# One burst of TensorE work per mLSTM chunk and per attention row block in a hybrid decoder layer on one Trainium2 core

## The chip, the cores and the metric

The kernel runs on one core of a Trainium2 chip. The core's engines work side by side, each through its own queue of instructions in order: TensorE (PE, matmuls and transposes into PSUM; PEld is its loading of weights), VectorE (DVE), ScalarE (ACT), GpSimd (POOL) and SyncE (SP, which issues all the DMAs here). The metric is the device time of one execution in microseconds, the median of the runs; lower is better. In a view, L81 is line 81 of the kernel.

## What is computed

One layer of a decoder over a sequence of 1024 tokens of width 1024, in float32. Two mixers, a differential attention (4 heads, causal, with a distance bias) and an mLSTM (4 heads, in chunks), read one projection of the normalised input; their outputs are gated, merged and projected back. Cut to what matters:

```python
h = _rmsnorm(x, norm_pre[l])
proj = jnp.einsum('bsd,dn->bsn', h, w_in[l])
qa, ka, va, za, qb, kb, vb, ob, zb, igb, fgb, ga, gb = _split(proj, sizes)
...
oa = _diff_attention(qa, ka, va, lam)
oa = _rmsnorm(oa, norm_a[l].reshape(H_A, 2 * HEAD_DIM_A)) * (1.0 - lam_init)
ya = oa.reshape(B, S, W_A) * jax.nn.silu(za)
...
qk = jax.nn.silu(_causal_conv(jnp.concatenate([qb, kb], axis=-1), conv_qk[l]))
hb = _mlstm(qb_c, kb_c, vb, ig, fg)
hb = jax.nn.sigmoid(ob.astype(jnp.float32)).reshape(B, S, H_B, HEAD_DIM_B) * hb
hb = _rmsnorm(hb, norm_b[l].reshape(H_B, HEAD_DIM_B)).astype(x.dtype)
yb = hb.reshape(B, S, W_B) * jax.nn.silu(zb)
merged = (jax.nn.sigmoid(ga) * jnp.einsum('bsw,wd->bsd', ya, w_a[l])
          + jax.nn.sigmoid(gb) * jnp.einsum('bsw,wd->bsd', yb, w_b[l]))
out = jnp.einsum('bsd,de->bse', merged, w_out[l])
x = x + _rmsnorm(out, norm_post[l])
```

Attention: per head two score matrices (queries and keys of 64 each), two softmaxes, `p0 - lam * p1`, then the product with the values. mLSTM: per chunk a decayed score matrix times the values, plus the queries times a running state C, and the update of that state.

## The kernel before, in words

Every float32 operand of the large products is split into a rounded part and a rest (`split`, L114: an ACT cast and a DVE subtraction), and a product takes three matmuls per 128 rows of depth. Small matmuls and all transposes are plain float32.

**Start (L163 to L218, L600 to L622).** WARM = 15 matmuls of ones run while the first loads are under way (L169). `npre` is the pre-norm weight vector on all 128 partitions; one DMA writes it there 128 times over (L172). Eight tiles of 128 tokens are loaded, normalised (`norm_tile`, L203: ACT square sum, DVE, a POOL power, DVE scaling by npre), transposed on PE (`turn_tile`, xT in the views) and split; `tok_pass` multiplies each by a first group of projection columns (`tok`). From tile 4 on, `turn_tile` also forms differences of the blocks, in PSUM's reach on DVE (t1, t2, L259) and, in `rest` (L262), two on POOL (L263, L264), whose splits are ht1 to ht4: the operands of a seven-product scheme of block multiplication.

**Products (L313 to L466).** The other projection columns are done in pairs of column blocks (`Pair`). Each pair needs seven products of 12 matmuls of 512 columns (`product`, L370), written to three PSUM accumulators, with ACT and DVE reading them out (`Banks.after`, L351) and preparing weights two products ahead (`prep`, L412). `run_pairs` (L431) walks over 24 pairs in a list (qkb: mLSTM queries and keys; qka: attention; ob, va: values and gates by token; zb, za, g: gates). In the views the tiles of a pair carry its name and the accumulator X, Y or Z. Behind the products of token-wise pairs, four transposes (tkT) are put off by one product by way of the list `later` (L454, L565). `merge_b` and `merge` (L1063) then multiply the mLSTM's outputs by w_b, 16 runs of 12 matmuls (mrg); the attention's outputs by w_a follow at the end, and then the output projection (out, L1192).

**Weaving (L1027 to L1050).** This product work, called the fill, is a generator: it yields the estimated time of each half product. The dependent chains, gate_chain, conv, mlstm and attn_head, are generators too and yield how much fill is wanted before they go on; `weave` pulls that much. `until(name)` pulls fill until a pair is done. A scheduler below the program may still move instructions a little; the built order is what counts.

**mLSTM (L783 to L887).** 32 chunks of 128 tokens. `lead` does the scores of the next chunk (sT, with kT a transpose of the keys), `follow` the current chunk's numerator and state update (num, upd), each followed by DVE and ACT work. Between lead and follow, and again behind follow, half of MSTEP = 7 us of fill is pulled. The causal convolution of the next head (`conv`, L743: six parts on DVE and ACT) is put behind chunks 2 to 5, one or two parts each.

**Attention (L927 to L1024).** Per head 8 row blocks of 128 queries. `score(i, c)` (two of them: matmuls S, a DVE pass that adds the bias and finds the minimum, L950, an ACT exponential, L957), `combine` (L966 to L971, DVE), `turn` (transposes pT on PE, copied by ACT, L987), `weigh` (pv on PE, read out by ACT, L996). Fill is pulled behind each of score 0, score 1 with combine, turn and weigh, in the parts FW = 1.0, 0.6, 1.3, 1.0 of a row block's share; row block i's turn and weigh come behind the scores of block i + 1. At a head's end POOL scales the rows (`scale_rows`, L719). A pool of five PSUM buffers (`misc`, L92) serves S, pT, pv, sT, kT, num, upd and the transposes.

## Time and profile before

| | us |
|---|---|
| median of 3 runs | 850.76 |
| lowest and highest run | 849.82, 855.57 |
| the profiled execution | 853.26 |
| its span, first to last instruction | 851.5 |
| PE busy in it | 830.5 |
| DVE, ACT, POOL busy in it | 571.5, 399.6, 63.2 |

The profile is of one execution. Busy time of PE counts matmuls whose ends overlap the next one's start, so it is an upper bound of what PE does. A wait is idle time of an engine just before an instruction, put down to what released it. The chain that ended last is followed back from the last instruction; its pieces are cut where the next begins. The granted clock of TensorE is shown as a share of full speed.

### The profile page before, as it was taken

How to read it: one execution, taken by the hardware profiler on the slowest of the kernel's cores; microseconds unless marked ns; L12 is line 12 of the kernel's file. 1: busy time of each engine (PE TensorE's matmuls, PEld its weight loads, DVE VectorE, ACT ScalarE, POOL GpSimd, SP SyncE). 2: the span in 40 equal slices, each digit the busy share in tenths (PEclk: the TensorE clock that was granted, in tenths of full speed). 3: DMA queues.
4: the chain of work that ended last, by engine and by line, in shares of the span. 5: the costliest groups of instructions: out<-in, count | busy, mean ns of one | idle time of the engine just before them, and what ended most of it. 6: DMA issues, size and time to landing. Idle time of an engine off the chain costs nothing.

```text
span 851.5 us, 12166 instructions
## 1 busy us (share of the span) xinstructions
PE 830.5 (98%) x4292; PEld 703.7 (83%) x4292; DVE 571.5 (67%) x1145; ACT 399.6 (47%) x890; POOL 63.2 (7%) x86
## 2 busy tenths in 40 slices
PE   7899999999999999999999999999999999999997
PEld 7898878888888888888888888788877888778885
DVE  6997868868757966666676765777576635782133
ACT  5554544545444544346555555565566422341110
POOL 1330000000000000100001000200200010000011
PEclk9999999999999999999999999999999999999999
DMA  7612433442452556563366416543567577940052
GB/s 267 200 38 76 124 100 105 142 145 76 127 161 75 169 165 188 171 188 123 112 177 198 132 63 205 178 125 99 192 231 255 178 257 258 307 153 1 1 197 99
DMA packets 100621, 128.96 MB, mean 151 GB/s; under 512 B 8680, under 2 KB 60112, under 8 KB 100560
## 3 DMA queue, kind: packets, MB, share of 16 engines
q1 hardware_dynamic: 100560, 128.18, 47.6%
q8 instruction: 34, 0.56, 0.3%
q14 instruction: 27, 0.22, 0.1%
HBM read 88.79 MB, written 39.35 MB: 150 GB/s over the span
## 4 chain that ended last, share of the span: by engine, by line
PE 76%; DVE 10%; DMA 8%; ACT 3%; issue 2%; SPq 1%; POOL 0%; DVEq 0%; POOLq 0%; ACTq 0%
PE out L81 10%; PE mrg L81 6%; PE pv L81 4%; PE S L81 3%; PE pT L84 2%; DMA zs<-z_d 2%; PE num L81 2%; PE tok L81 1%; PE qka1Y L81 1%; PE zb0Y L81 1%; PE g02Y L81 1%; PE za0Y L81 1%; PE g10Y L81 1%; PE qkb1Y L81 1%; PE qkb2Y L81 1%
## 5 line engine op out<-in xcount | busy, mean ns | idle before, releaser
L957 ACT ACTIVATE p<-p,ast 128x128 f32<-128x128 f32 (+7 forms) x64 | 49.7, 776 | 58.7 <-DVE ast L956 35.5
L950 DVE CUSTOM_DVE_ANT_0 p<-S,gm 128x384 f32<-128x384 f32 (+5 forms) x96 | 50.6, 553 | 22.2 <-PE S L81 21.7
L1211 DVE TENSOR_TENSOR o<-out,npost 128x512 f32<-128x512 f32 x16 | 11.1, 691 | 57.0 <-ACT oj L1207 57.0
L81 PE MATMUL mrg<-y,mbw 128*128 128x512 f32 x192 | 47.2, 395 | 0.0
L81 PE MATMUL mrg<-y,maw 128*128 128x512 f32 x192 | 44.0, 390 | 1.9 <-DVE tg L1084 1.9
L81 PEld LDWEIGHTS mrg<-y,maw 128*128 128x128 f32 x192 | 36.0, 188 | 9.7 <-DVE tg L1084 2.3
L1207 ACT ACTIVATE oj<-out 128x512 f32<-128x512 f32 x16 | 9.6, 598 | 69.3 <-PE out L81 69.2
L81 PEld LDWEIGHTS pv<-va,pT 128*128 128x128 f32 x288 | 36.8, 191 | 5.4 <-ACT pT L987 3.1
L81 PEld LDWEIGHTS mrg<-y,mbw 128*128 128x128 f32 x192 | 35.4, 188 | 6.9
L81 PE MATMUL pv<-va,pT 128*128 128x128 f32 x288 | 37.8, 276 | 1.3 <-ACT pT L987 1.2
L81 PE MATMUL S<-kll,qs 128*128 128x384 f32 (+5 forms) x96 | 32.7, 342 | 0.3 <-DMA kll<-qk_d 0.3
L1084 DVE SCALAR_TENSOR_TENSOR tg<-tg,mrg 128x512 f32<-128x512 f32 x32 | 21.9, 683 | 15.8 <-PE mrg L81 15.6
L81 PE MATMUL S<-khh,qs 128*128 128x384 f32 (+5 forms) x96 | 32.4, 340 | 0.0
L750 DVE SCALAR_TENSOR_TENSOR cv<-pad,cols,cv 128x1024 f32<-128x1024 f32 x24 | 30.7, 1280 | 0.1
L971 DVE SCALAR_TENSOR_TENSOR p<-p,ast,p 128x128 f32<-128x128 f32 (+7 forms) x32 | 26.2, 818 | 1.0
L81 PE MATMUL out<-wo,m 128*128 128x512 f32 x96 | 23.1, 389 | 0.0
L851 POOL TENSOR_TENSOR stb<-stb,mhalf 128x4 f32<-128x4 f32 x8 | 10.8, 1351 | 160.8 <-DVE stb L848 160.8
L115 ACT CAST m<-tg 128x512 fp32r<-128x512 f32 x16 | 9.9, 621 | 25.8 <-DVE tg L1155 25.8
L987 ACT COPY pT<-pT 128x512 f32<-128x512 f32 (+3 forms) x48 | 21.0, 472 | 2.0 <-PE pT L84 2.0
L81 PEld LDWEIGHTS S<-kll,qs 128*128 128x128 f32 x96 | 18.0, 188 | 3.8 <-DMA kll<-qk_d 0.5
L81 PEld LDWEIGHTS out<-wo,m 128*128 128x128 f32 x96 | 18.0, 188 | 3.7
L81 PE MATMUL out<-wot2h,m 128*128 128x512 f32 x64 | 21.0, 390 | 0.0
(1237 smaller groups left out, 2499.4 us busy)
## 6 DMA issues: line engine op xcount, KB each, us to landing
raw_g<-in_w_in_dram SPq DMA_DIRECT2D x16, 512.0 KB, 3.9
g_d<-g SPq DMA_DIRECT2D x32, 256.0 KB, 3.5
tg<-g_d SPq DMA_DIRECT2D x32, 256.0 KB, 3.9
raw_qkb<-in_w_in_dram SPq DMA_DIRECT2D x16, 256.0 KB, 3.3
z_d<-zt SPq DMA_DIRECT2D x16, 256.0 KB, 2.6
zs<-z_d SPq DMA_DIRECT2D x16, 256.0 KB, 4.6
raw_qka<-in_w_in_dram SPq DMA_DIRECT2D x16, 256.0 KB, 3.0
qk_d<-qah SPq DMA_DIRECT2D x16, 256.0 KB, 2.1
```

Source lines behind the costliest of these rows:

```text
L81: pin(nc.tensor.matmul(*args, **kw))
L84: pin(nc.tensor.transpose(out=out, in_=in_, identity=ident))
L115: nc.scalar.copy(hi, raw)
L750: nc.vector.scalar_tensor_tensor(out=cv, in0=pad[:, t : t + S], scalar=cols[:, t * 8 + blk : t * 8 + blk + 1], in1=cv, op0=ALU.mult, op1=A ...
L851: nc.gpsimd.tensor_tensor(rr, ss, mhalf[:, 0:4], ALU.pow)
L950: nc.vector.tensor_tensor_reduce(out=pr[:, n0:n1], in0=pss[:, : n1 - n0], in1=gm[:, (7 - i) * P + n0 : (7 - i) * P + n1], scale=-0.125, sc ...
L957: nc.scalar.activation(pr[:, :nk], pr[:, :nk], AF.Exp, bias=nm, scale=-1.0, accum_out=sth[:, c, i : i + 1],)
L971: nc.vector.scalar_tensor_tensor(out=p0[:, :nk], in0=p1[:, :nk], scalar=st[:, 3:4], in1=p0[:, :nk], op0=ALU.mult, op1=ALU.add,)
L987: nc.scalar.copy(pT[:, j0:j1], pt[:, 0 : (j1 - j0) * P].rearrange("p (j t) -> p j t", t=P))
L1084: nc.vector.scalar_tensor_tensor(out=tg, in0=tg, scalar=1.0, in1=ps, op0=ALU.add, op1=ALU.mult)
L1207: nc.scalar.activation(junk, ps, AF.Square, scale=D ** -0.5, accum_out=ssq[:, tt, cc : cc + 1])
L1211: nc.vector.tensor_mul(orr[:, c0 : c0 + 512], ps, npost[:, c0 : c0 + 512])
```

## The change

Six edits. (1) WARM goes from 15 to 8, and the pre-norm weights come as two rows of 512 on one partition, which PE spreads to 128 partitions by a matmul with ones and ACT copies to npre. (2) The two subtractions of `rest` go from POOL to DVE, and so does `scale_rows` of the attention. (3) Transposes put off by `later` wait for four product steps, or two at the next burst, where they join its work. (4) An mLSTM chunk does lead and follow together and then pulls all of its fill; the convolution has one part behind each of chunks 1 to 6. (5) A row block of the attention does weigh of block i - 2, turn of block i - 1 and both scores of block i together, and then pulls all of its fill; a head has ten such steps. (6) `weave` pulls at least 0.6 of what a chain wants, even where `until` has pulled ahead.

```diff
-WARM = 15
+WARM = 8
...
-LAST = 8
-FW = (1.0, 0.6, 1.3, 1.0)
+LAST = 5
...
-    nc.sync.dma_start(npre, norm_pre[0].partition_broadcast(P))
+    for n0 in range(0, D, 512):
+        prow, pn = temp("prow")[0:1, :], misc("npre")
+        nc.sync.dma_start(prow, norm_pre[:, n0 : n0 + 512])
+        nc.tensor.matmul(pn, ones[0:1, :], prow, start=True, stop=True)
+        nc.scalar.copy(npre[:, n0 : n0 + 512], pn)
...
         def rest():
-            nc.gpsimd.tensor_sub(b11, t2, b11)
-            nc.gpsimd.tensor_sub(b21, b21, t2)
+            nc.vector.tensor_sub(b11, t2, b11)
+            nc.vector.tensor_sub(b21, b21, t2)
...
-    later = []
+    fresh, later, tick = [], [], [0]
+
+    def turns(age):
+
+        while later and later[0][0] <= tick[0] - age:
+            later.pop(0)[1]()
...
-            flush, later[:] = later[:], []
             yield from pairs[p].run(i)
-            for f in flush:
-                f()
-            if finished:
-                done.add(finished)
-                finished = None
+            tick[0] = n
+            turns(4)
+            later.extend((n, f) for f in fresh)
+            fresh.clear()
             if i == 6:
-                finished = pairs[p].name
...
+                later.append((n, lambda name=pairs[p].name: done.add(name)))
+        tick[0] += 9
+        turns(0)
...
                 lead(*divmod(n + 1, NT))
-            yield w * 0.5
             follow(h, c)
...
-            if c % 4 == 1 and n > 4:
+            if c % 4 == 2 and n > 4:
...
-                if c == 2:
+                if c == 1:
                     until(f"qkb{h + 1}")
                     conv_next = conv(h + 1)
-                if 2 <= c <= 5:
-                    for _ in range(2 if c in (3, 5) else 1):
-                        next(conv_next, None)
-                if c == 5:
+                if 1 <= c <= 6:
+                    next(conv_next, None)
+                if c == 6:
                     drain(conv_next)
...
-            yield w * 0.5
+            yield w
...
-        unit = supply / FTOTAL
-        for i in range(NT + 1):
-            w = share(i) * unit
+        unit = supply / sum(share(i) for i in range(NT + 2))
+        for i in range(NT + 2):
+            if i > 1:
+                weigh(i - 2)
+            if 0 < i <= NT:
+                turn(i - 1)
             if i < NT:
                 score(i, 0)
-                yield w * FW[0]
                 score(i, 1)
                 combine(i)
-                if i == NT - 1:
-                    after()
-                yield w * FW[1]
-            if i > 0:
-                if i == 1 and before is not None:
-                    flip(*before)
-                turn(i - 1)
-                yield w * FW[2]
-                weigh(i - 1)
-                yield w * FW[3]
+            if i == 1 and before is not None:
+                flip(*before)
+            if i == NT - 1:
+                after()
+            yield share(i) * unit
...
-        scale_rows(raw, rr, nc.gpsimd)
+        scale_rows(raw, rr, nc.vector)
...
         for want in chain:
-            left[0] = pull(left[0] + want)
+            turns(2)
+            due = left[0] + want
+            now = max(due, 0.6 * want)
+            left[0] = pull(now) + due - now
```

How this moves the built order, first on PE in a chunk of the mLSTM's second head, before (kT, num: small work of the chunk; qkb2Y: products of the fill):

```order
L84 MATMUL kT<-ident,cv_1072 128x128
L81 MATMUL qkb2Y<-ht2h,qkb2w_1902 128x512
L81 MATMUL qkb2Y<-ht2l,qkb2w_1902 128x512
L81 MATMUL qkb2Y<-ht2h,qkb2w_1902 128x512 x2
L81 MATMUL qkb2Y<-ht2l,qkb2w_1902 128x512
L81 MATMUL qkb2Y<-ht2h,qkb2w_1902 128x512 x2
L81 MATMUL qkb2Y<-ht2l,qkb2w_1902 128x512
L81 MATMUL qkb2Y<-ht2h,qkb2w_1902 128x512 x2
L81 MATMUL qkb2Y<-ht2l,qkb2w_1902 128x512
L81 MATMUL qkb2Y<-ht2h,qkb2w_1902 128x512
L81 MATMUL num<-vbh,ring 128x129
L81 MATMUL num<-cn,qi 128x129
```

and the same kind of place with the change:

```order
L80 MATMUL qkb2Y<-ht4l,qkb2w_1992 128x512
L80 MATMUL qkb2Y<-ht4h,qkb2w_1992 128x512
L80 MATMUL sT<-cv_1073,cv_1074 128x128
L83 MATMUL kT<-ident,cv_1074 128x128
L80 MATMUL num<-vbh,ring 128x129
L80 MATMUL num<-cn,qi 128x129
L80 MATMUL upd<-vbh,ring 128x129
L80 MATMUL qkb2Y<-ht4h,qkb2w_1992 128x512
L80 MATMUL qkb2Y<-ht4l,qkb2w_1992 128x512
```

The twelve products that stood between kT and num are now on the two sides of one burst of sT, kT, num and upd.

On PE in the last head of the attention, sixth and seventh row block, before (S: scores, pT: transposes, pv: weighing, mrg: the fill):

```order
L81 MATMUL S<-khh_3_5918,qs_3_5916 128x448
L81 MATMUL S<-kll_3_5920,qs_3_5916 128x448
L81 MATMUL S<-khh_3_5918,qs_3_5916 128x448
L81 MATMUL S<-kll_3_5920,qs_3_5916 128x448
L81 MATMUL mrg<-y_6434,mbw_6588 128x512 x3
L81 MATMUL mrg<-y_6439,mbw_6588 128x512 x3
L84 MATMUL pT<-ident,p_6418 128x128 x6
L81 MATMUL mrg<-y_6444,mbw_6588 128x512 x3
L81 MATMUL mrg<-y_6449,mbw_6588 128x512 x3
L81 MATMUL mrg<-y_6434,mbw_6588 128x512 x3
L81 MATMUL mrg<-y_6439,mbw_6588 128x512 x3
L81 MATMUL pv<-va_5921,pT 128x128 x6
```

and with the change, one row block on:

```order
L80 MATMUL mrg<-y_6465,mbw_6562 128x512 x3
L80 MATMUL pv<-va_5909,pT 128x128 x6
L83 MATMUL pT<-ident,p_6512 128x128 x7
L80 MATMUL S<-khh_3_5905,qs_3_5903 128x512
L80 MATMUL S<-kll_3_5907,qs_3_5903 128x512
L80 MATMUL S<-khh_3_5905,qs_3_5903 128x512
L80 MATMUL S<-kll_3_5907,qs_3_5903 128x512
L80 MATMUL S<-khh_3_5906,qs_3_5904 128x512
L80 MATMUL S<-kll_3_5908,qs_3_5904 128x512
L80 MATMUL S<-khh_3_5906,qs_3_5904 128x512
L80 MATMUL S<-kll_3_5908,qs_3_5904 128x512
L80 MATMUL mrg<-y_6470,mbw_6562 128x512 x3
```

Scores, transposes and weighing, which had products between them, stand together, and each reads what the burst before it left.

On DVE at the start, about the third tile of tokens, before (x_171 and x_205: scaling by npre; ht1l: a split; gt, vb: reading out tok; scr: a small reduction):

```order
L260 TENSOR_TENSOR t_0_237<-xT_1_229,t_0_236 128x512
L217 TENSOR_SCALAR xst_208<-xst_208 128x1
L306 COPY vb_0_265<-tok 128x256
L635 ISA scr,lam_s<-scr 128x64
L635 ISA lam_s 128x1
L116 TENSOR_TENSOR ht1l<-t_0_236,ht1h 128x4x128
L220 SCALAR_TENSOR_TENSOR x_171<-x_171,xst_208,npre 128x1024
L217 TENSOR_SCALAR xst_300<-xst_300 128x1
L305 TENSOR_TENSOR gt<-tok,bif 128x8
L306 COPY vb_4_348<-tok 128x256
L220 SCALAR_TENSOR_TENSOR x_205<-x_205,xst_300,npre 128x1024
L116 TENSOR_TENSOR h11l<-xT_0_305,h11h 128x4x128
```

and with the change (x_173 and x_207 are the same tiles, b_0_203 and b_0_204 the subtractions that were POOL's):

```order
L309 COPY vb_0_267<-tok 128x256
L223 SCALAR_TENSOR_TENSOR x_173<-x_173,xst_210,npre 128x1024
L308 TENSOR_TENSOR gt<-tok,bif 128x8
L220 TENSOR_SCALAR xst_302<-xst_302 128x1
L309 COPY vb_4_350<-tok 128x256
L223 SCALAR_TENSOR_TENSOR x_207<-x_207,xst_302,npre 128x1024
L115 TENSOR_TENSOR h11l<-xT_0_307,h11h 128x4x128
L115 TENSOR_TENSOR h21l<-xT_1_314,h21h 128x4x128
L266 TENSOR_TENSOR b_0_203<-t_0_239,b_0_203 128x512
L267 TENSOR_TENSOR b_0_204<-b_0_204,t_0_239 128x512
L115 TENSOR_TENSOR ht2l<-t_0_239,ht2h 128x4x128
L115 TENSOR_TENSOR ht1l<-t_0_238,ht1h 128x4x128
```

The scaling of both next tiles moved ahead of the small reduction and of the split ht1l, and the two subtractions stand behind them.

## Rows read from the trace of the kernel before

**Rows 1.** The page, first part: busy us, share, instructions by engine.

```profile
PE 830.5 (98%) x4292; PEld 703.7 (83%) x4292; DVE 571.5 (67%) x1145; ACT 399.6 (47%) x890; POOL 63.2 (7%) x86
```

**Rows 2.** Waits of PE: engine, line, releaser, us in total, times, longest.

```profile
PE xT L84 <- DVE x L220: 2.5, 4, 0.9
PE mrg L81 <- DVE tg L1084: 1.9, 1, 1.9
PE xT L84 <- DVE xst L217: 1.6, 1, 1.6
PE tkT L84 <- DVE tk L548: 1.4, 2, 0.9
...
PE pv L81 <- ACT pT L987: 1.2, 2, 0.9
...
PE qka3X L81 <- DVE z L522: 0.8, 1, 0.8
```

**Rows 3.** Chain that ended last, 150 to 200 us: start us, us, what.

```profile
153.50 0.11 PE kT L84
153.60 2.79 PE g10Y L81 x12
...
156.84 0.22 PE upd L81 x2
157.06 2.76 PE zb0Y L81 x12
159.83 2.72 PE g10X L81 x12
...
172.89 2.73 PE g10Z L81 x12
```

**Rows 4.** Busy us of each engine in stretches: stretch, length, engines, clock, DMA, GB/s.

```profile
8.00:10.00 2.00, 1.31 (x8) 0.84 (x8) 0.89 (x2) 0.66 (x1) 0.00 (x0) 1.00 1.13 334
8.28:57.00 48.72, 43.41 (x353) 41.69 (x354) 43.98 (x69) 31.32 (x59) 12.86 (x14) 1.00 0.56 179
370.00:695.00 325.00, 322.06 (x1680) 272.32 (x1679) 221.02 (x522) 184.02 (x432) 17.23 (x12) 1.00 0.53 169
```

**Rows 5.** Timeline of the start: start us, us, engine, line, operation, idle before.

```profile
1.10 6.25 PE L170 MATMUL warm<-ones 128*128 128x128 f32 x30 [1.10 <-DVE mprev L695]
...
1.70 0.42 SPq L172 DMA_DIRECT2D npre<-in_norm_pre_dram  x1
...
7.48 1.41 DVE L220 SCALAR_TENSOR_TENSOR x<-x,xst,npre 128x512 f32<-128x512 f32 x2 [2.21 <-DMA npre<-in_norm_pre_dram]
8.28 1.32 PE L84 MATMUL xT<-ident,x 128*128 128x128 f32 x8 [0.94 <-DVE x L220]
...
9.34 1.07 ACT L115 CAST wc<-raw_c 128x1056 fp32r<-128x1056 f32 x1 [5.20 <-DMA raw_c<-in_w_in_dram]
...
10.95 0.75 PE L81 MATMUL tok<-wc,h11h 128*128 128x264 f32 x4 [1.35 <-ACT h11h L115]
```

**Rows 6.** DMA issues to 25 us: operands, queue, count, KB each, us to landing.

```profile
x<-in_x_dram SPq DMA_DIRECT2D x2, 256.0 KB, 2.7
```

**Rows 7.** Timeline of DVE and POOL at 35 us.

```profile
34.54 0.69 DVE L260 TENSOR_TENSOR t<-xT,t 128x512 f32<-128x512 f32 x1
...
35.38 1.30 POOL L263 TENSOR_TENSOR b<-t,b 128x512 f32<-128x512 f32 x1 [3.99 <-DVE t L260]
35.48 1.74 DVE L116 TENSOR_TENSOR ht1l<-t,ht1h 128x512 fp32r<-128x512 f32 x1
```

**Rows 8.** Groups by form, 370 to 695 us: busy us, mean ns of one, idle before.

```profile
L950 DVE CUSTOM_DVE_ANT_0 p<-S,gm 128x512 f32<-128x512 f32 x24 | 15.9, 687 | 2.2 <-PE S L81 2.0
L987 ACT COPY pT<-pT 128x512 f32<-128x512 f32 x24 | 13.4, 577 | 2.0 <-PE pT L84 2.0
...
L957 ACT ACTIVATE p<-p,ast 128x1024 f32<-128x1024 f32 x8 | 9.2, 1153 | 11.6 <-DVE ast L956 11.6
...
L971 DVE SCALAR_TENSOR_TENSOR p<-p,ast,p 128x1024 f32<-128x1024 f32 x4 | 5.1, 1284 | 0.1
```

## What I predict

> **What bounds the kernel now.** I read the page's shares first, then PE's waits, the chain that ended last, a table by stretch, and the timelines of the start. The shares show PE busy 98% of the span and DVE 67% [rows 1]: PE is the bound, but its busy time counts overlapping matmuls, so it does not say what can be won. PE's waits do. The reader is to see how little they are: 2.5 and 1.6 us for xT, 1.9 for the merge, 1.4 for tkT, 1.2 for pv, 0.8 for qka3X are the main ones in a span of 851.5 [rows 2]. The rest is matmul work that the change leaves in place: in the built order PE has the same products, transposes and small matmuls, less 7 warm-ups and plus the two that spread the row. A gain can only come from these waits, from what it costs PE to leave a product stream and come back, and from the start. The chain shows the second: twelve products take 2.72 us where nothing cuts in, 2.79 behind sT and kT, 2.76 behind num and upd [rows 3]. By stretch, DVE is the full engine at the start, 43.98 of the 48.72 us between the first transpose and 57 us, and has a third of its time free in the attention stretch, 221.02 of 325 us busy [rows 4].
>
> The sum is made against the profiled execution: 853.26 us, its span of 851.5 and 1.8 around it. That lies 2.5 above the median of the runs, 850.76, and I take the gain off the median.
>
> **The start: the weights as a row.** Today the broadcast of norm_pre is issued at 1.70 and DVE can use it at 7.48; PE begins xT at 8.28, and the first tok waits until 10.95 because ACT's cast of wc begins only at 9.34, when raw_c has landed [rows 5]. The broadcast writes 128 x 1024 x 4 bytes, 512 KB, and the queues then run at 334 GB/s [rows 4]: without it raw_c lands 1.5 us sooner, less some 0.3 because SP issues two transfers where one of 0.42 stood [rows 5]. The row itself is two transfers of 2 KB behind two of x, which land 2.7 us after issue [rows 6]: at about 1.7 + 2.7 = 4.4. Then come two matmuls of two passes. At the pace of the warm-up, 6.25 / 30 = 0.21 a pass where kT's pass later takes 0.11 [rows 3, 5], a pass of 512 columns takes twice the 2.72 / 12 = 0.227 of a product, so 4 x 0.45 = 1.8; two ACT copies follow, 0.6 each (pT's copy of that shape, [rows 8]). First half near 6.0, second near 7.0, xT near 7.1 instead of 8.28. Eight warm-ups end at 1.1 + 16 x 0.21 = 4.5 and hold nothing up. Both ways I get 1.2. Bounds: if the row lands no sooner than the broadcast does today (7.48), xT comes at 9.7 and 1.4 is lost; at best raw_c's 1.5 and the ACT order give 2.0. **Term: -1.2.**
>
> **Subtractions from POOL to DVE.** Eight subtractions of 128x512 leave POOL. While POOL does one, DVE's split of ht1l takes 1.74 us, where DVE's own subtraction of that size just ahead takes 0.69 [rows 7]; the timeline of the start has eight such stretched pieces, 8 x 1.05 = 8.4. On DVE the subtractions cost 8 x 0.69 = 5.5. So DVE, the fuller engine there, gains 2.9, and in its new order the scaling of the next x stands ahead of the splits. PE loses 2.5 + 1.6 = 4.1 on xT [rows 2], of which 0.9 belongs to the start counted above: 3.2 are left and I take three quarters, 2.4. Bounds: 3.2, or a loss of 5.5 - 2.9 = 2.6 if half of the stretching has another cause and PE follows DVE. **Term: -2.4.** The scaling of the attention rows moves to DVE too (8 x 0.69 = 5.5); I cost it at nothing, since DVE has 104 us free in that stretch [rows 4]; without that cover it is 5.5.
>
> **One burst instead of several.** In the built order PE leaves the product stream 192 times before and 95 times after: once a chunk instead of twice, once a row block instead of four times. A burst costs 0.07, 0.04 or 0.01 in the three cases of [rows 3] (2.79, 2.76 and 2.73 against 2.72); I take 0.035 as nearest to most rows of that view. 97 x 0.035 = 3.4. Bounds 97 x 0.01 = 1.0 and 97 x 0.07 = 6.8. **Term: -3.4.**
>
> The Trainium skill speaks against this term: "TensorE: Matmul & The Clock Gate", Part 2, has PE pull weight loads ahead of the matmuls in flight, so that work of another kind in between should not break the stream. By that rule the term is 0. The trace agrees in the main, for a burst shows 0.01 to 0.07 only, but not to the end.
>
> **Waits that the new order loosens.** A token tile's transposes now run two product steps or more behind the DVE sum that they read, before only one: tkT's 1.4 go [rows 2]. A row block's weighing now stands a whole burst behind the copy of its transposes, before 1.3 parts of the row block's 3.9: pv's 1.2 go. Late next in both places is nothing that the waits list. **Terms: -1.4 and -1.2.** The convolution in six equal parts shifts DVE work between chunks and removes none, and no wait of PE names it: 0, bounds -0.7 and +1.
>
> **What a burst adds.** A row block's scores now have a single gap until their transposes, and ACT and DVE get everything at once. For the longest row block DVE has four pieces of 0.69, ACT an exponential of 1.15 behind the last, DVE then the combination of 1.28 [rows 8]. DVE falls behind PE by about 1.4 in those four, so the chain behind the last score is 1.4 + 1.15 + 1.28 and some 0.8 of small ones, 4.6 us. In the built order the narrowest such gap (third head) holds 24 products, 24 x 0.227 = 5.4; in the first and last head 36, 8.2. So 0.8 of room at worst, on a DVE that is two thirds busy and whose splits for the products stand behind the combination. I take +0.6, one wait like qka3X's 0.8 [rows 2] less some room. Bounds 0 and +13 (rival 4). The five PSUM buffers of that pool must serve up to seven tiles in a burst; the sixth waits for pv's two copies of 128 columns, each no longer than the 0.58 of 512 columns [rows 8], while eight transposes (8 x 0.11) and two score pieces (4 x 0.227) lie between, 1.8 against 1.2, so nothing is added. **Term: +0.6.**
>
> The merge's 1.9 keeps its cause, a DVE that stands behind a transfer, and the change only shifts it: 0, bounds -1.9 and +2.
>
> Sum: -1.2 - 2.4 - 3.4 - 1.4 - 1.2 + 0.6 = -9.0. The profiled execution would come to 844.3, the median to 850.76 - 9.0 = **841.8**, 1.06% less. About 1% is what a measurement of this kernel can tell from no change, so the forecast sits just beyond that border, 842.3.
>
> **Rivals.**
> 1. More goes than I count: qka3X and the merge too (0.8 + 1.9), and the burst adds nothing (0.6): 841.8 - 3.3 = 838.5. For it: both are DVE being late [rows 2], and DVE is relieved. Against: the order of the merge is no simpler than before. Chance 0.2.
> 2. Coming back to a stream is free, and what looks like its cost belongs to the products: 841.8 + 3.4 = 845.2, within 1%. For it: 0.07 and 0.01 stand side by side for like bursts. Chance 0.13.
> 3. The clock rises later. PE now works without a pause from 1.10 for 6.25 us; its passes there take 0.21, the level of 1.2 GHz, and later ones 0.11, that of 2.4 GHz [rows 3, 5]. With 8 warm-ups it may pause between 4.5 and 7.1. If some 40 passes of tok and xT then run at half pace, 40 x 0.11 = 4.4, a third of it beside waits: +3, 844.8. Against: the two spreading matmuls fill most of the pause. Chance 0.08. The Trainium skill, same page, Part 1, has the lower level as the default that activity releases; by that rule this rival is possible, and no run here shows it yet.
> 4. Slower: the lumps. DVE waits in order for both exponentials, the splits for the products come late, and behind each row block a product waits. The place is the attention stretch with its 32 row blocks; at half of qka3X's 0.8 [rows 2] each, 32 x 0.4 = 12.8 instead of 0.6: 841.8 + 12.2 = 854.0. From 0.3 a block the change is slower than before, from 0.57 by over 1%. Against: a third of DVE is free there [rows 4]. Chance 0.12, half of it beyond 1%.
>
> **How the numbers follow.** The forecast has 0.47 and a range of its own of 838.5 to 846, across the border: 0.29 below it, 0.18 above. Faster by over 1%: 0.29 + 0.2 (rival 1) + 0.03 (rivals 2 and 3 where the start gives its 2.0 and the burst nothing) = 0.52. Slower by over 1%: 0.06. Within 1%: 0.42. The range goes down to rival 1 with the best cases of the start and of xT (838.5 less 2.5), 836, and up to where rival 4 has taken most of the gain, 849.5.
>
> **What would show it.** The lines of tkT and pv leave PE's waits and the xT lines shrink from 4.1 to about 1. The first xT comes near 7.1, the first tok near 9.7. DVE's split of ht1l takes 0.69. In the chain most runs of twelve products are whole. New lines of pT or S waiting for DVE, or of products waiting for a split, with over 5 us together, mean rival 4; passes of 0.21 us beyond 8 us mean rival 3; xT lines still at 4 mean that the term of the subtractions was wrong.

## The result, and the profile after

| | before | after |
|---|---|---|
| median, us | 850.88 | 845.65 |
| lowest and highest of 6 runs | 849.82, 855.57 | 845.01, 847.18 |
| the profiled execution | 853.26 | 845.01 |
| its span | 851.5 | 843.3 |

The ratio of after to before is 0.9927, with a 95% interval of 0.9909 to 0.9945: faster by 0.7%, within the 1% that was called no change, inside the predicted range, 3.85 us above the predicted time. (It lies near the ratio of the means of the six runs, 851.9 and 845.9, about 6 us apart; the medians are 5.2 apart.) The two profiled executions differ by 8.25 us, 3 more than the medians, because the one of before lies 2.4 above its median and the one of after is its kernel's fastest run. So a difference between these two profiles has to be held against more profiles before it is believed, and the experiments gave those. One profiled execution of them (four_bursts) ran at a granted clock of 0.65 from end to end and took 1185.11 us; nothing is read from it.

The page of after, busy time by engine, answers to [rows 1]:

```profile
PE 828.1 (98%) x4282; PEld 705.7 (84%) x4282; DVE 571.8 (68%) x1161; ACT 401.1 (48%) x892; POOL 38.4 (5%) x70
```

POOL has lost 25 us of work, and DVE carries 16 instructions more in the same busy time (571.5 before): what the subtractions and scalings cost it, it gets back from pieces that are no longer stretched. The waits of PE after, beside [rows 2] (engine, line, releaser, us in total, times, longest; around the helpers the line numbers are one less than before):

```profile
PE pT L83 <- DVE p L970: 3.4, 3, 1.5
PE mrg L80 <- DVE tg L1083: 1.8, 1, 1.8
PE out L80 <- DVE wot2l L115: 1.8, 2, 1.3
PE warm L169 <- DVE mprev L699: 1.1, 1, 1.1
PE xT L83 <- DVE x L223: 0.4, 1, 0.4
```

The reader is to see three lines gone (tkT, pv, qka3X), xT down from 4.1 to 0.4, and one new line: pT waits 3.4 for DVE's combination.

The timeline of the start (start us, us, engine, line, operation, idle before), beside [rows 5]:

```profile
1.10 3.78 PE L169 MATMUL warm<-ones 128*128 128x128 f32 x16 [1.10 <-DVE mprev L699]
1.70 0.59 SPq L173 DMA_DIRECT2D prow<-in_norm_pre_dram  x2
4.81 3.78 PE L174 MATMUL npre<-prow,ones 1*128 1x512 f32 x4
7.60 0.75 DVE L223 SCALAR_TENSOR_TENSOR x<-x,xst,npre 128x512 f32<-128x512 f32 x1 [2.33 <-ACT npre L175]
8.52 1.11 PE L83 MATMUL xT<-ident,x 128*128 128x128 f32 x4
9.10 1.07 ACT L114 CAST wc<-raw_c 128x1056 fp32r<-128x1056 f32 x1
10.82 1.23 PE L80 MATMUL tok<-wc,h11h 128*128 128x264 f32 x4
```

The row is there in time (the spreading starts at 4.81), but its four passes take 3.78 us, and the first xT comes at 8.52, later than the 8.28 of before. ACT's cast of wc waits for no transfer any more and comes at 9.10 all the same.

DVE at 35 us, beside [rows 7]: the subtraction that was POOL's (L266), and the split ht1l.

```profile
34.84 0.68 DVE L266 TENSOR_TENSOR b<-t,b 128x512 f32<-128x512 f32 x1
...
39.71 0.68 DVE L115 TENSOR_TENSOR ht1l<-t,ht1h 128x512 fp32r<-128x512 f32 x1
```

The split takes 0.68 where it took 1.74 beside POOL. Three instructions on PE cut the span into stretches that hold the same work in every kernel here (start, middle, merge and rest in the table): the first product, the first product with w_a, and the first output product. In after they start at:

```profile
65.14 0.50 PE L80 MATMUL qkb0Y<-h11h,qkb0w 128*128 128x512 f32 x1
...
701.95 13.31 PE L80 MATMUL mrg<-y,maw 128*128 128x512 f32 x58
...
747.57 0.39 PE L80 MATMUL out<-wo21h,m 128*128 128x512 f32 x1
```

The same three rows of every profile, subtracted, give this table (us; "rest" is the span less the third start). The ratios are those to the kernel before, with 95% intervals:

| kernel | ratio | interval | start | middle | merge | rest |
|---|---|---|---|---|---|---|
| before | 1 | | 68.72 | 642.32 | 45.71 | 94.75 |
| before_again | | | 68.42 | 641.23 | 44.80 | 94.75 |
| after | 0.9927 | 0.9909 to 0.9945 | 65.14 | 636.81 | 45.62 | 95.73 |
| start_back | 0.9927 | 0.9909 to 0.9944 | 66.03 | 637.52 | 47.94 | 94.91 |
| subs_pool | 0.9964 | 0.9950 to 0.9977 | 68.49 | 637.39 | 48.41 | 95.11 |
| rows_pool | 0.9905 | 0.9884 to 0.9925 | 63.84 | 634.64 | 48.25 | 95.17 |
| burst_only | 0.9952 | 0.9933 to 0.9970 | 69.00 | 636.05 | 49.73 | 94.12 |
| four_again | 0.9939 | 0.9920 to 0.9957 | 63.71 | 639.87 | 44.64 | 95.88 |
| attn_parts | 0.9914 | 0.9894 to 0.9934 | 65.17 | 642.17 | 44.02 | 95.64 |
| parts_rows | 0.9887 | 0.9868 to 0.9907 | 63.52 | 638.11 | 43.86 | 95.91 |
| rows_merge | 0.9862 | 0.9839 to 0.9886 | 65.97 | 635.89 | 45.64 | 95.60 |
| parts_merge | 0.9856 | 0.9835 to 0.9877 | 63.70 | 636.16 | 43.52 | 93.32 |
| merge_fb16 | 0.9839 | 0.9820 to 0.9857 | 64.37 | 636.04 | 43.52 | 93.37 |

A ratio of 0.001 is 0.85 us; an interval reaches some 1.6 us to each side, so the time alone does not tell effects under 2 us apart, and the columns do so only where several profiles agree. Two profiles of the same code can differ by 2.0 us in the middle and by some 2 in the rest.

### The profile page after: what moved, and what is told of

Read it like the earlier page. It is cut to its first block, busy times and chain, and to the rows that moved or that the text cites. A ratio compares the mean times of both kernels' runs of the same rounds, so it can differ in the third digit from the quotient of the medians.

```text
span 843.3 us, 12218 instructions
## 1 busy us (share of the span) xinstructions
PE 828.1 (98%) x4282; PEld 705.7 (84%) x4282; DVE 571.8 (68%) x1161; ACT 401.1 (48%) x892; POOL 38.4 (5%) x70
## 4 chain that ended last, share of the span: by engine, by line
PE 84%; DMA 7%; DVE 4%; ACT 2%; issue 2%; SPq 1%; POOL 0%; DVEq 0%; POOLq 0%; ACTq 0%
PE out L80 10%; PE tok L80 6%; PE S L80 4%; PE pv L80 3%; DMA m_d<-tg 3%; PE mrg L80 2%; PE pT L83 2%; PE num L80 1%; DMA zs<-z_d 1%; PE qkb0Y L80 1%; PE g04Y L80 1%; PE g00Y L80 1%; PE za1Y L80 1%; PE g02Y L80 1%; PE g12Y L80 1%
## 5 line engine op out<-in xcount | busy, mean ns | idle before, releaser
L80 PE MATMUL mrg<-y,mbw 128*128 128x512 f32 x192 | 44.9, 391 | 0.0
L80 PE MATMUL S<-khh,qs 128*128 128x384 f32 (+5 forms) x96 | 34.7, 367 | 0.0
L823 ACT ACTIVATE junk<-raw 128x128 bf16<-128x128 f32 x32 | 9.9, 310 | 32.3 <-DVE raw L818 32.1
L83 PE MATMUL pT<-ident,p 128*128 128x128 f32 x144 | 21.2, 274 | 3.5 <-DVE p L970 3.4
L995 ACT ACTIVATE oa<-pv 128x128 f32<-128x128 f32 x32 | 8.9, 277 | 30.9 <-PE pv L80 30.8
```

The source lines that it names most:

```text
L80: pin(nc.tensor.matmul(*args, **kw))
L83: pin(nc.tensor.transpose(out=out, in_=in_, identity=ident))
L823: nc.scalar.activation(junk, raw[:, c, 0:P], AF.Square, accum_out=stbs[h, c // 4][:, 1, c % 4 : c % 4 + 1])
```

## The experiments

### The start alone: start_back and subs_pool

start_back puts the broadcast and the 15 warm-ups back, subs_pool the two subtractions.

```diff
-WARM = 8
+WARM = 15
...
-    for n0 in range(0, D, 512):
...
+    nc.sync.dma_start(npre, norm_pre[0].partition_broadcast(P))
```

> The kernel after, with 15 warm-up matmuls and the broadcast of the pre-norm weights by DMA, as before. In the profile after, the first transpose xT comes at 8.52 us (before: 8.28) and the first tok at 10.82 (before: 10.95). Theory: the row is worth nothing by itself, so this kernel takes as long as the kernel after, 845.65 +-0.6, and first xT comes near 8.3. Rival (the step of the prediction): the row is worth 1.2 us by the DMA time that it frees, this kernel takes 846.9 or more, and its last tok lies 1.2 us later than the 64.75 of after.

Measured: ratio 0.9927, that of after, and the first xT at 7.98. In time the row is worth 0, to within some 2 us, as the theory had it, which leaves the rival's 1.2 open. The theory's reason does not hold, though: eight profiles have the row and the subtractions on DVE, and they fall into two kinds. In three (after, attn_parts, rows_merge) the spreading takes 3.78 us and the first product comes at 65.1 to 66.0. In five it takes 1.98 to 2.33, and the first product comes at 63.5 to 64.4; rows_pool, with the same start in its code, is one of these:

```profile
4.81 2.27 PE L174 MATMUL npre<-prow,ones 1*128 1x512 f32 x4
7.75 1.67 PE L83 MATMUL xT<-ident,x 128*128 128x128 f32 x8 [0.67 <-DVE x L223]
9.40 1.25 PE L80 MATMUL tok<-wc,h11h 128*128 128x264 f32 x4
```

The mean of the eight is 64.4, against 66.03 in the one profile of start_back: by that one reference the row gives 1.6, of the predicted size, but between 0.1 and 2.5 by the execution. A single profile would have settled on either end. The other pair gives less: where POOL has the subtractions, the first product comes at 69.00 without the row (burst_only) and at 68.49 with it (subs_pool), and at 68.42 and 68.72 in the two profiles of before. So the row shows a gain only where the subtractions are on DVE, and its size stays open.

```diff
-            nc.vector.tensor_sub(b11, t2, b11)
-            nc.vector.tensor_sub(b21, b21, t2)
+            nc.gpsimd.tensor_sub(b11, t2, b11)
+            nc.gpsimd.tensor_sub(b21, b21, t2)
```

> The kernel after, with the two subtractions of rest back on POOL. Theory: the whole 3.6 us by which the last tok of after comes sooner (64.75 against 68.33 us) is theirs, so it takes 3.5 us more than the kernel after, 849.1, and DVE's split of ht1l is back at some 1.7 us beside POOL's subtraction. Rival A (the prediction's term): 2.4 more, 848.0. Rival B: the gain at the start comes from the row, and this kernel takes no longer than the kernel after.

Measured: 0.9964, 3.2 us above after, and the stretched pieces are back (POOL's two subtractions and DVE's splits beside them):

```profile
35.14 1.30 POOL L266 TENSOR_TENSOR b<-t,b 128x512 f32<-128x512 f32 x1 [3.98 <-ACT ht1h L114]
35.25 1.73 DVE L115 TENSOR_TENSOR ht1l<-t,ht1h 128x512 fp32r<-128x512 f32 x1
36.40 1.74 POOL L267 TENSOR_TENSOR b<-b,t 128x512 f32<-128x512 f32 x1
36.91 1.77 DVE L115 TENSOR_TENSOR ht2l<-t,ht2h 128x512 fp32r<-128x512 f32 x1
```

With POOL's subtractions the first product stands at 68.4 to 69.0 in all four profiles, with DVE's at 63.5 to 66.0 in all nine. Rival B is out. The time does not decide between the theory's 3.5 and the prediction's 2.4 (3.2, with an interval of some 1.2 to 5.1); the table gives 3.0 (69.00 to 66.03 without the row) and 3.4 (68.49 to 65.14 with it). "SBUF — State Buffer" of the Trainium skill, section "SBUF: two separate sides", has VectorE and GpSimd share one pair of ports that one instruction holds to its end; the trace agrees that a split with two operands waits beside POOL, and prices it at 1.05 of POOL's 1.30.

### scale_rows: rows_pool

```diff
-        scale_rows(raw, rr, nc.vector)
+        scale_rows(raw, rr, nc.gpsimd)
```

> The kernel after, with scale_rows of the attention back on POOL. In the profile after, DVE waits 1.75 us at a head's end for POOL's power of the row norms (540.87 us) with the next head's score pieces queued behind it, and PE waits 1.62 us for the first row block's transposes at 544.1. Theory: on POOL the scaling holds no queue that PE needs, so this kernel is faster than the kernel after by 1 to 1.7 us, some 844.3, and the wait at 544 is gone. Rival: the wait there is made by the narrow gap of 12 products alone, or POOL's four multiplications slow DVE beside them, and the time stays at 845.6 or grows.

Measured: 0.9905, 1.9 us below after; attn_parts against parts_rows is the same edit in the old order of the attention, 2.3. Each alone is within its interval; both agree, and their mean, 2.1, is just clear of zero (some 0.4 to 3.7). The wait of pT falls from 3.4 to 1.2: with the bursts it is 2.8 to 3.4 in the three profiles with the scaling on DVE (after, start_back, subs_pool) and 1.2 to 1.6 in the three with it on POOL (rows_pool, burst_only, rows_merge). At the end of the second head, in after (POOL's power, the scaling, the first row block's transposes):

```profile
539.20 1.64 POOL L1018 TENSOR_TENSOR sth<-sth,mhalf 128x8 f32<-128x8 f32 x1 [32.76 <-DVE sth L1015]
...
540.87 1.29 DVE L726 TENSOR_TENSOR oa<-oa,sth 128x512 f32<-128x512 f32 x2 [1.75 <-POOL sth L1018]
...
543.28 0.28 DVE L949 CUSTOM_DVE_ANT_0 p<-S,gm 128x128 f32<-128x128 f32 x1
...
545.90 0.30 PE L83 MATMUL pT<-ident,p 128*128 128x128 f32 x1 [1.46 <-DVE p L970]
```

and in rows_pool:

```profile
538.57 2.70 POOL L726 TENSOR_TENSOR oa<-oa,sth 128x512 f32<-128x512 f32 x2
...
538.95 1.42 DVE L115 TENSOR_TENSOR qal<-qa,qah 128x512 fp32r<-128x512 f32 x1
...
542.48 0.30 PE L83 MATMUL pT<-ident,p 128*128 128x128 f32 x1 [0.38 <-DVE p L970]
```

On POOL the scaling stretches one split of DVE, from 0.68 to 1.42. On DVE it costs 1.29 and, ahead of that, 1.75 in which DVE waits in order for POOL's power, with a read-out (qa), a split and the next head's score pieces queued behind. The scaling still depends on POOL; only its place in a queue has changed.

### The bursts together: burst_only

The edits of start_back, subs_pool and rows_pool together.

> The kernel after with the start, the subtractions and scale_rows as before: only the bursts, the put-off transposes, the convolution in six parts and the pulling rule of the change are left. The prediction's terms for these are -3.4 - 1.4 - 1.2 + 0.6 = -5.4, so 845.4. Theory after the result: new waits at the first row blocks of a head (3.4 us for pT in the profile after) take most of that, and with the start's 3.6 us taken off the measured gain of 5.2 some 1.6 is left: 849.2. Rival: coming back to a product stream is free (-0), then the loosened waits -2.6 and the new ones +3.4 give 851.6, no gain at all.

Measured: 0.9952, 4.1 us below before (2.6 to 5.7). The rival (no gain) is out; the prediction's 5.4 lies inside the interval, the 1.6 that the new waits were to leave does not. The middle falls from 641.8 (mean of the two profiles of before) to 636.05, and the merge rises from 45.3 to 49.73.

### What one burst costs: four_bursts, four_again

An mLSTM chunk with four pieces of the fill, behind sT, kT, num and upd (lead and follow each yield once inside, which is left out here):

```diff
-                lead(*divmod(n + 1, NT))
-            follow(h, c)
+                for _ in lead(*divmod(n + 1, NT)):
+                    yield w * 0.25
+            yield w * 0.25
+            for _ in follow(h, c):
+                yield w * 0.25
...
```

> The kernel after, with the fill of an mLSTM chunk pulled in four quarters: behind sT, kT, num and upd of the chunk. In the built order PE then leaves the product stream 183 times instead of 95; the attention and the start are as in the kernel after. Theory (the prediction's 0.035 a burst): 88 x 0.035 = 3.1 us more than the kernel after, so a ratio to before near 0.996, and 10 to 15 fewer matmuls between 69 and 371 us than the 1505 of after, all of it in bursts that take longer than their matmuls. Rival (coming back to a stream is free): the time of the kernel after, ratio 0.993, and 1500 or more matmuls in that stretch.

> four_bursts once more, unchanged: its first profiled execution ran at a granted clock of 0.65 from end to end, so that its trace can't be set beside the others, and its time, ratio 0.9942 with an interval of 0.9923 to 0.9961, lies between the theory's 0.9963 (88 bursts at 0.035) and the rival's 0.9927 (a burst costs nothing). Theory: in the trace some 1490 to 1495 matmuls between 69 and 371 us, against 1505 in the kernel after, 3 us, and the time comes at 0.995 to 0.996. Rival: 1500 or more, and 0.993. A third way: the stretch shows the 3 us, but the time does not, because what PE loses there it would have waited for later.

Measured: 0.9942 and 0.9939. Busy time of PE and PEld between 69 and 371 us (stretch, length, each engine's busy us with its instructions, granted clock, DMA share, GB/s), after and then four_again:

```profile
69.00:371.00 302.00, 302.00 (x1505) 254.70 (x1504) 222.34 (x417) 144.38 (x318) 12.06 (x17) 1.00 0.43 130
```

```profile
69.00:371.00 302.00, 301.92 (x1493) 251.44 (x1492) 220.87 (x415) 144.08 (x316) 12.53 (x17) 1.00 0.44 130
```

Twelve matmuls fewer fit in, and this is not scatter: the ten profiles with one burst a chunk, after among them, all have 1502 to 1505 there. The middle takes 2.6 us more than the 637.2 that after, start_back and subs_pool show on the mean: 88 bursts at 0.03, which is the prediction's size (0.035). In time 1.0 to 1.3 of it are seen, with intervals that hold both 0 and 3, and four_again's merge is 1 to 4 us shorter than those of the same three kernels. That fits the third way, but one profile cannot show it. What the prediction drew from the Trainium skill ("TensorE: Matmul & The Clock Gate", Part 2: weight loads are pulled ahead of the matmuls in flight), namely that a burst would be free, is not borne out to the end by this stretch.

### The attention's bursts: attn_parts, parts_rows

The attention's loop of before put back (score 0, score 1 with combine, turn, weigh, each with its part of the fill), once with scale_rows on DVE and once on POOL.

```diff
-            yield share(i) * unit
+                yield w * FW[0]
...
+                yield w * FW[3]
```

> The kernel after, with the attention's order as before: score 0, score 1 with combine, turn and weigh each followed by its part of the fill, weighing in the same step as turning. 176 bursts instead of 95. Theory: 81 x 0.035 = 2.8 us come back and the wait of pv for its copies (1.2 before) too, while the new waits of pT (3.4) go: +0.6, so a time within 1.5 us of the kernel after, ratio 0.993 to 0.995. Rival: the attention's bursts are a net loss, because what they add at the narrow gaps is more than what they save, and this kernel is faster than the kernel after by 2 us or more (ratio 0.991 or less). Second rival, the prediction as it stands (2.8 + 1.2 - 0.6): slower by 3.4, ratio 0.997.

> The attention's order as before (as in attn_parts) and scale_rows on POOL: beside rows_pool (ratio 0.9905) it prices the attention's bursts alone, and beside attn_parts (0.9914) the place of scale_rows in the old order. Theory: scale_rows on DVE costs only where a short row block stands alone in front of a burst, so here its place is worth nothing and the ratio stays at 0.991; the bursts of the attention are then worth some 0.8 us net. Rival: on DVE it costs 1.9 us in any order, this kernel comes to 0.989, faster than rows_pool, and the attention's bursts are a loss of 1 us. Second rival (the prediction's 2.8 + 1.2 for bursts and pv): slower than rows_pool by 4 us, 0.995.

Measured: 0.9914 and 0.9887, against 0.9927 and 0.9905 with bursts. The 3.4 us that the prediction's terms give for the attention (2.8 + 1.2 - 0.6) are excluded; in time its bursts are worth something between a gain of 1 us and a loss of some 3. The first rival of parts_rows is right in its first half (the place of scale_rows costs 2.3 here too); that the bursts are a loss, the intervals leave open. One wait is traded for another: pv for its copies against pT for the combination. The waits of parts_rows:

```profile
PE out L81 <- DVE wot2l L116: 2.0, 2, 1.3
PE pv L81 <- ACT pT L990: 1.4, 3, 0.7
```

In the middle the old order takes 638.11 and, with the same code there, 636.16 (parts_merge); the burst form with POOL's scaling 634.64 to 636.05. On the mean that is 1.5 us saved there (637.1 against 635.7 in four profiles), less than the 2.0 by which the two of the old order differ. attn_parts' 642.17 holds a wait of 2.3 and a fall of the clock behind it (below).

### The merge: rows_merge, parts_merge, merge_fb16

In after's last merge, ACT's cast of the output weights waits 5.15 us for its transfer, DVE's split stands behind the cast, the read-out tg behind the split, and PE behind tg:

```profile
713.96 1.05 ACT L114 CAST wo21h<-raw_o 128x1024 fp32r<-128x1024 f32 x1 [5.15 <-DMA raw_o<-in_w_out_dram]
...
715.04 1.22 DVE L115 TENSOR_TENSOR wo21l<-raw_o,wo21h 128x1024 fp32r<-128x1024 f32 x1 [4.15 <-ACT wo21h L114]
716.19 0.68 DVE L115 TENSOR_TENSOR m<-tg,m 128x512 fp32r<-128x512 f32 x1
716.79 0.68 DVE L1083 SCALAR_TENSOR_TENSOR tg<-tg,mrg 128x512 f32<-128x512 f32 x1
...
717.52 4.83 PE L80 MATMUL mrg<-y,maw 128*128 128x512 f32 x20 [1.81 <-DVE tg L1083]
```

How late that cast comes sets the wait. It starts 12.0 us behind the first product with w_a in after, 12.8 to 13.2 in start_back, rows_pool, subs_pool and burst_only, and 10.2 to 10.4 in four_again, attn_parts and parts_rows; in each of the eight, PE's wait for tg behind it is this time less 10.2, to within 0.2 (1.8, 2.6 to 3.0, and 0 to 0.2). What makes the cast late is not tested: the transfer is issued 4.8 to 9.1 us behind that product and its cast starts 4.1 to 6.1 us later.

rows_merge, parts_merge and merge_fb16 load and split the first two pieces inside the merge.

```diff
-    drain(merge("ma", w_a_v, 0, ys_a, finish_a))
+    for n, _ in enumerate(merge("ma", w_a_v, 0, ys_a, finish_a)):
+        if n == 7:
+            first_raws = [out_raw(0, 0, g) for g in range(2)]
+        if n == 15:
+            out_weights(0, 0, first_raws)
...
```

> rows_pool, and the first two pieces of the output weights are loaded and split inside the last merge (behind its second and fourth column block) instead of behind it. In every profile so far DVE stands behind a cast of such a piece that waits for its transfer, and PE waits 1.8 to 3.0 us for DVE's read-out of mrg; in four of the six profiles the granted clock falls after that wait (0.76 in rows_pool between 715 and 722 us). Theory: the wait and the loss of clock behind it go, 3 to 5 us less than rows_pool, ratio 0.985 to 0.987. Rival: the transfers are late wherever they stand, or another of the merge's transfers takes the wait over, and the ratio stays at 0.9905.

Measured: 0.9862, 3.7 us below rows_pool, as the theory had it (with an interval of some 1.0 to 6.3), though its profiled execution, the slowest of its six runs, still shows a wait of the merge:

```profile
PE mrg L80 <- DVE tg L1083: 2.2, 3, 1.3
PE out L80 <- DVE wot2l L115: 1.7, 2, 1.3
```

> parts_rows (the attention's order as before, scale_rows on POOL) with the early output weights of rows_merge. In the profiles the attention's bursts save 3 us between the first product qkb0Y and the first w_a product (638.11 us in parts_rows, 634.64 in rows_pool), and rows_pool gives 4.4 back between there and the first out (43.87 against 48.25), because the first piece of the output weights reaches ACT at 711.8 and 711.5 us in both. Theory: in the old order PE comes late enough for that transfer, so loading it early brings nothing here: ratio 0.9887 as in parts_rows, 2 us more than rows_merge (0.9862); the bursts' gain shows once the transfer is out of the way. Rival: the early load is worth its 3.7 us in any order, and this kernel comes to 0.9845.

Measured: 0.9856, 2.6 us below parts_rows (with an interval of some 0.2 to 5.1): the rival is nearer, and the theory's nothing lies just outside. I had taken it that the attention's bursts save 3 us which the transfer takes back. By the times the early load helps in the old order too, though parts_rows shows no wait for mrg. Of the 4.7 us between the two spans 2.6 lie in the rest: the pieces that follow come earlier too, the first split of wot2l begins 2.5 us behind the first out in parts_rows and 0.6 ahead of it in parts_merge, and the waits of out for it, 2.0, are gone. This does not come with the edit every time: in rows_merge, which has the same edit, that split begins 2.2 behind the first out, and out waits 1.7. Another 2.0 lie in the middle, where the code is the same: scatter between executions. With the early load the two orders of the attention can't be told apart (0.9862 and 0.9856).

```diff
-FB = 8
+FB = 16
```

> rows_merge with FB = 16 instead of 8, so that the first row blocks of a head get more of the fill and the last ones less (shares 16 to 23 instead of 8 to 15). Theory: the waits of pT for DVE (1.6 us in the profile of rows_merge) belong to the short gaps of the first row blocks and go, up to 1.5 us less than rows_merge, ratio 0.9845. Rival: the longest row blocks, whose gap gets smaller, wait in their place, and the ratio stays at 0.986 or rises.

Measured: 0.9839, 838.98 us, the fastest kernel here, 0.9% below after. Against rows_merge it gains 2.0, within the two intervals. The theory's reason does not hold, though. The waits of pT fall from 1.6 to 0.9, S takes over 1.5 at other places, and the middle, where the shares act, is as long as in rows_merge (636.04 and 635.89). What the profile has gained stands in the other three columns, where the code is the same: 1.6 in the start, 2.1 in the merge, 2.2 in the rest. So a gain from FB is not shown.

```profile
PE S L80 <- ACT oa L996: 1.0, 1, 1.0
PE pT L83 <- DVE p L970: 0.9, 2, 0.5
...
PE S L80 <- DVE y L580: 0.5, 1, 0.5
```

### What is typical of before: before_again

> The kernel before, unchanged, for a second profile. Theory: its waits at xT, tok, tkT and pv are those of the first profile within 0.5 us each, so the terms rest on what is typical; the merge's wait may differ, and where it is 2.5 us or more the granted clock falls behind it as in the changed kernels. Rival: the waits of tkT and pv (1.4 and 1.2) belong to one execution, and the second profile lacks them.

Measured: 850.94 us. The waits of pv (1.5) and xT and tok are as in the first profile; tkT shows 0.6 instead of 1.4, and the merge 1.0 instead of 1.9, with no fall of the clock. So the term for tkT rested partly on one execution. The put-off transposes and the pulling rule have no experiment of their own; no profile with them shows a wait of tkT.

## Why the prediction came out as it did

The time was in the range, the sum too large: -9.0 against -6.2 by the ratio (-5.2 by the medians). By its own terms:

- **The weights as a row, -1.2.** Open: -1.6 on the mean of eight profiles against the one of start_back, -0.5 in the pair with POOL's subtractions, and nothing that the times can tell. What the prediction got wrong here is the pace of the spreading: "4 x 0.45 = 1.8" is nearly met in two profiles (1.98 in parts_rows and merge_fb16), less so in rows_pool (2.27), and not in after (3.78). Its first xT "near 7.1" and first tok "near 9.7" come at 7.28 and 8.84 in parts_rows, 7.75 and 9.40 in rows_pool, 8.52 and 10.82 in after.
- **Subtractions to DVE, -2.4.** Right in mechanism, if anything a little small: 3.2 in time, 3.0 and 3.4 in the start. The xT lines went to 0.4, where about 1 was forecast.
- **scale_rows at nothing.** Wrong, and the first of two steps that failed. The cover, a DVE free for a third of the stretch, was real but not at that place: the instruction waits there for POOL with other work queued behind it. It cost 1.9 and 2.3 in the two pairs, 1.7 in the middle (637.2 against 635.5, the mean of rows_pool, rows_merge and burst_only).
- **Bursts, -3.4, and the loosened waits, -1.4 and -1.2, less 0.6.** Together -5.4. The middle gives -6.2 where POOL scales (641.8 to 635.5) and -4.5 where DVE does. The price of a burst was right in the mLSTM (0.03). The sum hides errors inside: tkT was 0.6 in another execution, and the attention's share was put too high (3.4 by the terms, at most 1 by the times). "Most runs of twelve products are whole" is not met either: in after's chain from 150 to 200 us runs of twelve (2.72 to 2.74) and halves of six, on the two sides of a burst, alternate.
- **What a burst adds, +0.6.** Too small: pT waits 3.4 in after, 2.2 of it by way of scale_rows. The prediction priced the longest row block, but the waits of after stand at short ones: 1.46 and 1.05 at the first two row blocks of the third head (the longest at 545.90, above), behind the scaling of the old head, and 0.92 at the third row block of the first head, where no scaling stands ahead.
- **The merge at 0, bounds -1.9 and +2.** The second step that failed. "The change only shifts it" is not what the profiles show: burst_only, subs_pool, start_back and rows_pool take 47.9 to 49.7 in the merge, the two of before 44.8 and 45.7; only after itself, at 45.6, and four_again, at 44.6, do not. The six average 47.4, +2.2. In the four the longest wait for tg is 2.6 to 3.0, in before 1.9 and 1.0, and behind the longer ones PE also ran slower for some us: the 132 matmuls that follow the wait take 30.22 in after and 31.79 to 33.10 in the four. For the other five runs of after this is inferred from these kernels, not seen.

Put together from several kernels: -4.1 at the start (64.4 against 68.6), -4.5 in the middle, +2.2 in the merge and +0.3 in the rest (94.75 before, 95.0 on the mean of after, start_back, subs_pool, rows_pool and burst_only) make -6.1, the size that was measured. The one profile of after, its fastest run, gives -3.4, -5.0, +0.4 and +1.0 against the means of the two of before, -7.1; that the agreement of the first sum is so close is partly luck.

Of the rivals, the first (more waits go) fell with the merge. The second (a free return) gave 845.2, nearest to the result, but for the wrong reason: four_again shows the cost. The third (a later clock) can't be laid to the change. The first tok takes 1.23 to 1.25 instead of 0.75 in after and in rows_pool, but the start of before shows the same in other executions: 1.25 for the first tok of burst_only and for the second of before_again, where the granted clock is 0.50 between 12 and 14 us. The first product came sooner all the same, with PE's waits at xT down from 4.1 to 0.4. The prediction's sign for it, passes of 0.21 us, was read off the lengths alone: the record of before grants 1.00 in the warm-up too. The fourth (slower by lumps) fell: its waits add up to 3.4, not 12.8.

## What to carry to other kernels

An instruction moved to an engine with free time costs nothing only if its inputs are there when its turn in that engine's queue comes; look up who produces them and what stands behind it before its cost is set to zero. When PE arrives sooner, look at the first place where a transfer sets the pace, because the gain can be given back there, and load that operand earlier in the same edit. For gains under 1% take several profiles and compare stretches that hold the same work: here one profile of each kernel showed 8.25 us where the medians showed 5.2.

## What the runs showed of the hardware that I had not expected

**The same start runs at two paces.** Four passes of the spreading take 3.78 us in one execution and 2.27 in another of the same code. The passes of tok behind them are slow in both. The view by stretch of rows_pool has a granted clock of 0.50, the level of 1.2 GHz, just there, after it had been 1.00 up to 8 us; in after the record says 1.00 through the same 2 us, with tok at the same slow 1.23. Here are rows_pool and then after:

```profile
10.00:12.00 2.00, 1.84 (x8) 1.53 (x8) 2.00 (x4) 2.00 (x5) 0.00 (x0) 0.50 1.09 373
```

```profile
10.00:12.00 2.00, 1.95 (x8) 1.69 (x8) 1.79 (x3) 2.00 (x4) 0.00 (x0) 1.00 1.11 380
```

The fall and the slow tok do not come from the change: burst_only, with the start of before, has both (the first fence is its clock from 12 to 14 us, the second its first tok):

```profile
12.00:14.00 2.00, 1.84 (x8) 1.53 (x8) 2.00 (x3) 2.00 (x5) 0.00 (x0) 0.50 0.97 310
```

```profile
11.19 1.25 PE L80 MATMUL tok<-wc,h11h 128*128 128x264 f32 x4 [1.38 <-ACT h11h L114]
```

At the start the length of a pass and the recorded clock can disagree, so both have to be read; which of them is right in after, no run shows.

**A wait can cost twice.** Behind after's wait of 1.81 in the merge the granted clock was 1.00 and 22 matmuls took the next 5.0 us. Behind rows_pool's wait of 2.81 it was 0.76 over 7 us:

```profile
715.05 7.13 PE L80 MATMUL mrg<-y,maw 128*128 128x512 f32 x23 [2.81 <-DVE tg L1083]
```

```profile
715.00:722.00 7.00, 6.95 (x23) 5.55 (x24) 5.06 (x8) 3.23 (x5) 0.00 (x0) 0.76 0.81 267
```

So a wait of 2.8 was followed by a loss of some 2 us more, and the waits of 2.6 to 3.0 in start_back, subs_pool and burst_only by granted clocks of 0.50 to 0.66 in stretches of 4 us, while the merge shows no fall behind waits of 1.0 to 1.9. The same was seen behind attn_parts' wait of 2.3 for pv (0.54 over the next 3.7 us). "TensorE: Matmul & The Clock Gate" of the Trainium skill, Part 1, names the lower level as the default that work releases; the fall behind waits agrees with it.
